# Two raw tiles and six weight slots in place of three and five, in the feed-forward stages of a decoder trunk

## The chip, the cores and the metric

The kernel runs on one core of a Trainium2 chip. The metric is the device time of one execution in microseconds; lower is better. The time of a kernel is the median of its runs. Times inside an execution come from one profiled execution and are counted from the start of its span.

PE is the matmul engine (TensorE), DVE VectorE, ACT ScalarE, POOL GpSimd, and SP the engine whose queue issues most of the DMAs. Each engine works through its own instructions in a fixed order.

## The reference

Two decoder layers over 256 positions of width 2048. Layer 0 mixes with sliding-window attention beside an mLSTM memory, layer 1 with a forgetting attention. Each layer then has a SwiGLU feed-forward stage with 5632 hidden columns, which is what this change touches:

```python
h = h + mix.astype(h.dtype)
h = h + swiglu(rms_norm(h, norm_ffn[layer]), w_gate[layer], w_up[layer], w_down[layer])

def swiglu(xn, w_gate, w_up, w_down):
    return (jax.nn.silu(xn @ w_gate) * (xn @ w_up)) @ w_down
```

All inputs are float32.

## The kernel before

**Split products.** A float32 operand is split in two parts, `hi` (a cast by ACT to the matmul's own format) and `lo` (the rest, a subtraction by DVE). A product is then three matmuls, hi x hi, hi x lo and lo x hi (`three`, L557 to L559, and L244 to L246 in `gemm`). Every weight is loaded once from HBM by SP into a raw tile (L145), cast by ACT and subtracted by DVE into a weight slot, and read by PE from there.

**Plain pairs and seven-product pairs.** A feed-forward stage works in groups (`pair_group`): two weight blocks of 512 columns at a time, gate and up or two neighbouring blocks of the down weight, over a list of pairs of 128 input rows. The list `ORDER` gives the kind of each pair by position: 0, 2, 4, 6 and 7 are plain, 1, 3 and 5 are seven-product pairs. A plain pair takes two raw tiles of two blocks (128x1024, tag `raw`, four buffers), two weight slots and 24 matmuls. A seven-product pair treats rows, columns and halves of the positions as a 2x2 block product and forms it with seven block products (Strassen-Winograd) instead of eight: 21 matmuls, but more work on DVE. Its four blocks come into one raw tile of four blocks (`quad()`, L638). Three of them are split straight into a `triple` (ACT's cast of 128x1536 at L380, DVE's `lo` at L381; there are two triples); then DVE forms differences in place in the raw tile (L645, L648, L649), and the results go by two more splits (128x1024 each) into two weight slots, `h1` and `h0` (L650 to L652). The raw tile is read last by the subtraction for `h0`.

**Slots and raw tiles.** Outside the feed-forward stage, the pool `wp` (six buffers, tag `hi`) gives weight slots one at a time. For the stage, `close_layer` takes all six: five go into `stock`, around which `slot()` goes in turn, and the sixth, `own` (L807), serves as a four-block raw tile. Two more raw tiles (`QUADS`, tag `quad`) stand in the stage's own pool; `quads` is the ring of the three, with `own` first. So the first seven-product pair of each layer uses `own`, the second and third the two other tiles. One buffer with tag `quad` first holds a block of the residual stream that is transposed by DMA (`scrap`, n = 1, L374).

**What stands before the stage.** `out_proj` (L535) computes the output projection in four column blocks; its weight chunks use the same six slots. Each finished block is added to the residual stream (`add_out`, L395), copied by ACT (L338), transposed by SP's DMA (L340), joined by ACT (L345) and split into the stage's input `xh`, `xl` (L386, L387). The joins of the last two blocks are issued inside the first group of the stage, behind the cast of the pairs at positions 3 and 5 (`LATER`, `run_due`).

**Order.** The order of each engine's instructions is not written out by hand. The program gives a priority (its own order), and a planner that runs a model of the machine's timeline puts each instruction where the model finds its inputs and buffers ready. So a tile that is free early may be loaded early. After that the order is fixed.

Of the kernel before, what the change touches and what calls it, by code (L numbers as in the profile page):

```python
# [7 lines left out]
F32 = mybir.dt.float32  # L8
BF16 = mybir.dt.bfloat16
F32R = mybir.dt.float32r  # L10
# [7 lines left out]
P = 128  # L18
# [5 lines left out]
NB = 512  # L24
CK = 2
# [29 lines left out]
QUADS = 2  # L55
# [13 lines left out]
def mixed_of(order):  # L69
    return [p for w, p in order if w]  # L70
# [5 lines left out]
def trunk(  # L76
# [26 lines left out]
    wp = ctx.enter_context(tc.tile_pool(name="wp", bufs=6))  # L103
    stock, triples, quads = [], [], []

    def slot():
        if not stock:
            both = wp.tile([P, 2, CK, NB], F32R, tag="hi", name="hi")
            return [both[:, a, :, :] for a in range(2)]
        stock.append(stock.pop(0))  # L110
        return stock[-1]
# [423 lines left out]
    def out_proj(w, idx, key, extra):  # L535
        last, rest = KT - 4, []
        for n0 in (0, 2):
            accs = [new_acc() for _ in range(2)]
            for i in range(2):
                gemm(accs[i], m_of, w, (n0 + i) * NB, NB, 0, last, KT, step=6 * i)  # L540
            for i in range(2):
                gemm(accs[i], m_of, w, (n0 + i) * NB, NB, last, KT, KT, step=6)
                add_out(accs[i], n0 + i)
                (later if n0 == 0 else rest).append(
                    (LATER[n0 + i], split_turned(idx, n0 + i, *scrap(extra[3], n0 + i), extra))
                )
                square_sum(key, n0 + i)
        return rest
# [247 lines left out]
    def close_layer(layer, w_out, idx, key, **rest):  # L796
        with tc.tile_pool(name=f"fp{layer}", bufs=2) as fp:
            junk_of[:] = fp, "tmp", 2
            nx = len(mixed_of(ORDER))
            nd = max(len(mixed_of(o)) for o in DOWN.values())  # L800
            sx = [fp.tile([P, nx, 4, P], F32R, name=f"sx{i}", bufs=1) for i in range(2)]
            x4 = fp.tile([P, 2, P], F32R, name="x4", bufs=1)
            todo = out_proj(w_out, idx, key, (*sx, x4, fp))
            sd = [fp.tile([P, nd, 4, P], F32R, tag=f"sd{i}", name=f"sd{i}", bufs=1) for i in range(2)]
            triples.extend([fp.tile([P, 3, NB], F32R, name=f"{a}{i}", bufs=1) for a in ("hi", "lo")] for i in range(2))
            stock.extend([slot() for _ in range(5)])
            own = wp.tile([P, 2, CK, NB], F32R, tag="hi", name="raw").rearrange("p a k n -> p (a k) n").bitcast(F32)  # L807
            quads.extend([own] + [fp.tile([P, 2 * CK, NB], F32, tag="quad", name="raw", bufs=QUADS) for _ in range(QUADS)])
            ffn(layer, fp, sx, x4, sd, key, todo, **rest)
            stock.clear()  # L810
            triples.clear()
            quads.clear()
# [3 lines left out]
    hi, lo = slot()  # L816
# [368 lines left out]
    for n in range(4):  # L1185
        nc.gpsimd.dma_start(h[:, :, n * NB : (n + 1) * NB], xv[:, :, n * NB : (n + 1) * NB])

    close_layer(0, w_out_even[0], 2, "f0", idx_next=1, key_next="m1")


    r1 = rstd("m1")
    wi1 = w_in_odd[0]
    with tc.tile_pool(name="od", bufs=1) as od:
# [80 lines left out]
        for i in range(4):  # L1274
# [23 lines left out]
            elif i < 3:  # L1298
                n = NB if i == 1 else VT
# [32 lines left out]
    def finish(acc, n, gf):  # L1332
        for t in range(NT):
# [31 lines left out]
            nc.scalar.dma_start(ov[:, t, NB : 2 * NB], b1)  # L1365

    close_layer(1, w_out_odd[0], 3, "f1", finish=finish)


# [47 lines left out]
```

## Time and profile before

| | us |
|---|---|
| median of 3 runs | 2092.7 (2092.03 to 2093.31) |
| profiled execution | 2090.63 |
| its span | 2088.8 |
| PE busy | 2072.2 (99%) |
| DVE busy | 1806.2 (86%) |
| ACT busy | 1368.3 (66%) |
| span, feed-forward stage of layer 0, first product matmul | 328.03 |
| the same, layer 1: start of the first cast for it on ACT that PE waits for | 1389.82 |

A row of a timeline gives start, length, engine, line, operation, the tiles written and read, shapes, and a count where equal instructions are joined; in brackets stands the idle time of the engine before it and what ended it. Busy time of PE is modelled from pipelined matmuls, each shown some 0.39 us long though the next one starts 0.23 us after it; where PE runs without a stop is seen from the distance between starts. "SPq" is the issue of a DMA by SP, not its transfer.

### The profile page before, as it was taken

The numbers are of one execution on the slowest core, as the hardware profiler recorded it, in microseconds if no ns is written. First come the engines' busy times: TensorE is split into PE (matmuls) and PEld (weight loads), VectorE is DVE, ScalarE is ACT, GpSimd is POOL, SyncE is SP. The second block draws the span as 40 slices with busy tenths as digits, with TensorE's granted clock in tenths as the row PEclk, the third lists the DMA queues.
The fourth block names the chain that finished last, engine by engine and source line by source line (L and its number), as shares of the span: only waits on it lengthen the run. The fifth ranks groups of instructions, "written<-read, shape, count | busy, mean of one in ns | idle before, by whom it ended". The sixth has DMA issues, their size and how long they took to land.

```text
span 2088.8 us, 26467 instructions
## 1 busy us (share of the span) xinstructions
PE 2072.2 (99%) x9473; PEld 1715.1 (82%) x9473; DVE 1806.2 (86%) x2169; ACT 1368.3 (66%) x1649; POOL 44.1 (2%) x69
## 2 busy tenths in 40 slices
PE   9999999999999999999999999999999999999998
PEld 7878887888888888888888888878888888888887
DVE  6788767999999989998899688679989999999984
ACT  6777677665577646667677676577655667556763
POOL 1010000000000000000000001000000000000000
PEclk9999999999999999999999999999999999999999
DMA  8566577766677666666676776586756766666754
GB/s 292 175 206 195 189 240 195 236 205 197 206 216 229 211 193 223 219 209 185 204 205 214 223 202 183 156 255 217 237 186 196 232 197 217 226 206 200 235 157 159
DMA packets 309571, 434.84 MB, mean 208 GB/s; under 512 B 106412, under 2 KB 114624, under 8 KB 309312
## 3 DMA queue, kind: packets, MB, share of 16 engines
q1 hardware_dynamic: 307088, 426.27, 65.3%
q0 software_dynamic: 1632, 5.80, 0.9%
q8 instruction: 74, 1.21, 0.2%
q10 hardware_dynamic: 720, 1.09, 0.1%
q14 instruction: 57, 0.47, 0.1%
HBM read 408.68 MB, written 2.12 MB: 197 GB/s over the span
## 4 chain that ended last, share of the span: by engine, by line
PE 91%; ACT 3%; DMA 2%; DVE 2%; issue 1%; SPq 0%; POOL 0%; POOLq 0%; ACTq 0%; DVEq 0%
PE acc L558 21%; PE acc L557 20%; PE acc L559 20%; PE prod L557 5%; PE prod L558 5%; PE prod L559 5%; PE acc L245 4%; PE acc L244 4%; PE acc L246 4%; PE p L411 1%; ACT box L345 1%; DMA box<-box 1%; DVE hi L207 1%; PE po L512 0%; DMA raw<-in_w_up_dram 0%
## 5 line engine op out<-in xcount | busy, mean ns | idle before, releaser
L206 ACT CAST hi<-raw 128x1024 fp32r<-128x1024 f32 (+3 forms) x561 | 568.2, 1025 | 361.6 <-PE acc L559 194.3
L207 DVE TENSOR_TENSOR hi<-raw,hi 128x1024 fp32r<-128x1024 f32 (+3 forms) x561 | 659.4, 1188 | 129.2 <-ACT hi L206 127.1
L559 PE MATMUL acc<-hi,xl 128*128 128x512 f32 x1320 | 512.4, 390 | 0.0
L557 PE MATMUL acc<-hi,xh 128*128 128x512 f32 x1320 | 495.8, 391 | 4.8 <-ACT hi L206 4.5
L380 ACT CAST hi<-raw 128x1024 fp32r<-128x1024 f32 (+2 forms) x299 | 345.8, 1170 | 230.4 <-PE acc L559 195.1
L558 PE MATMUL acc<-hi,xh 128*128 128x512 f32 x1254 | 487.7, 390 | 0.4 <-DVE hi L207 0.4
L557 PEld LDWEIGHTS acc<-hi,xh 128*128 128x128 f32 x1320 | 247.5, 188 | 58.7 <-ACT hi L206 6.2
L559 PEld LDWEIGHTS acc<-hi,xl 128*128 128x128 f32 x1320 | 247.9, 188 | 51.7
L558 PEld LDWEIGHTS acc<-hi,xh 128*128 128x128 f32 x1254 | 235.5, 188 | 49.9 <-DVE hi L207 0.8
L381 DVE TENSOR_TENSOR hi<-raw,hi 128x1024 fp32r<-128x1024 f32 (+1 forms) x204 | 241.2, 1183 | 10.1 <-ACT hi L380 9.3
L381 DVE TENSOR_TENSOR lo<-raw,hi 128x1536 fp32r<-128x1536 f32 x95 | 166.8, 1755 | 48.1 <-ACT hi L380 46.0
L559 PE MATMUL acc<-hi,ml 128*128 128x512 f32 x466 | 181.0, 389 | 0.0
L557 PE MATMUL acc<-hi,mh 128*128 128x512 f32 x466 | 173.2, 389 | 0.0
L558 PE MATMUL acc<-hi,mh 128*128 128x512 f32 x437 | 170.4, 390 | 0.1
L245 PE MATMUL acc<-hi,mh 128*128 128x512 f32 (+1 forms) x322 | 126.3, 392 | 0.0
L244 PE MATMUL acc<-hi,mh 128*128 128x512 f32 (+1 forms) x322 | 125.8, 391 | 0.0
L246 PE MATMUL acc<-hi,ml 128*128 128x512 f32 (+1 forms) x322 | 123.7, 391 | 0.0
L645 DVE TENSOR_TENSOR raw<-raw 128x1024 f32<-128x1024 f32 x95 | 115.8, 1219 | 0.3
L557 PEld LDWEIGHTS acc<-hi,mh 128*128 128x128 f32 x466 | 87.5, 188 | 18.2
L559 PEld LDWEIGHTS acc<-hi,ml 128*128 128x128 f32 x466 | 87.5, 188 | 18.1
L245 PE MATMUL acc<-hi,xh 128*128 128x512 f32 (+3 forms) x288 | 99.9, 347 | 0.2 <-DVE hi L207 0.2
L246 PE MATMUL acc<-hi,xl 128*128 128x512 f32 (+3 forms) x288 | 99.1, 345 | 0.0
(364 smaller groups left out, 3077.8 us busy)
## 6 DMA issues: line engine op xcount, KB each, us to landing
raw<-in_w_gate_dram SPq DMA_DIRECT2D x176, 512.0 KB, 4.3
raw<-in_w_up_dram SPq DMA_DIRECT2D x176, 512.0 KB, 4.8
raw<-in_w_down_dram SPq DMA_DIRECT2D x176, 512.0 KB, 4.7
raw<-in_w_in_odd_dram SPq DMA_DIRECT2D x88, 512.0 KB, 5.1
raw<-in_w_in_even_dram SPq DMA_DIRECT2D x51, 512.0 KB, 4.8
raw<-in_w_out_even_dram SPq DMA_DIRECT2D x32, 512.0 KB, 5.0
raw<-in_w_out_odd_dram SPq DMA_DIRECT2D x32, 512.0 KB, 4.8
hr<-in_w_in_even_dram SPq DMA_DIRECT2D x12, 512.0 KB, 4.4
```

The source lines that it names most:

```text
L206: latest[0] = nc.scalar.copy(hi[:, k, 0:n], raw[:, k, 0:n])
L207: nc.vector.tensor_tensor(out=lo[:, k, 0:n], in0=raw[:, k, 0:n], in1=hi[:, k, 0:n].bitcast(F32), op=ALU.subtract)
L244: nc.tensor.matmul(o, ah[:, ts], hi, start=(k == 0), stop=False)
L245: nc.tensor.matmul(o, ah[:, ts], lo, start=False, stop=False)
L246: nc.tensor.matmul(o, al[:, ts], hi, start=False, stop=(k == k_all - 1 and cs.stop == n))
L345: nc.scalar.copy(ju[:, :, b], turned[:, b, :, :, :].rearrange("p k t q -> p (k t q)"))
L380: cast = nc.scalar.copy(dst_h, src)
L381: nc.vector.tensor_tensor(out=dst_l, in0=src, in1=dst_h.bitcast(F32), op=ALU.subtract)
L557: nc.tensor.matmul(o, ah, hi, start=start, stop=False)
L558: nc.tensor.matmul(o, ah, lo, start=False, stop=False)
L559: nc.tensor.matmul(o, al, hi, start=False, stop=stop)
L645: nc.vector.tensor_tensor(out=raw[:, 1:4:2, :], in0=raw[:, 3:4, :].broadcast_to([P, 2, NB]), in1=raw[:, 1:3, :], op=ALU.subtract)
```

## The change

`own` goes: the sixth buffer of `wp` becomes a sixth weight slot in `stock`, and the ring of four-block raw tiles has the two of the stage's pool alone. The first seven-product pair takes the first of these, the second pair the second, the third pair the first again, and so on.

```diff
-            stock.extend([slot() for _ in range(5)])
-            own = wp.tile([P, 2, CK, NB], F32R, tag="hi", name="raw").rearrange("p a k n -> p (a k) n").bitcast(F32)
-            quads.extend([own] + [fp.tile([P, 2 * CK, NB], F32, tag="quad", name="raw", bufs=QUADS) for _ in range(QUADS)])
+            stock.extend([slot() for _ in range(6)])
+            quads.extend(fp.tile([P, 2 * CK, NB], F32, tag="quad", name="raw", bufs=QUADS) for _ in range(QUADS))
```

No instruction is added or taken away, and no tile changes its size.

## The prediction

> **What bounds the kernel now.** I read the page first, then the waits of the matmul engine (PE), the table of stretches, and last the timelines of PE, the sync queue (SP), ScalarE (ACT) and VectorE (DVE) where PE is not full. From the page:
>
> ```profile
> span 2088.8 us, 26467 instructions
> ...
> PE 2072.2 (99%) x9473; PEld 1715.1 (82%) x9473; DVE 1806.2 (86%) x2169; ACT 1368.3 (66%) x1649; POOL 44.1 (2%) x69
> ...
> PE 91%; ACT 3%; DMA 2%; DVE 2%; issue 1%; SPq 0%; POOL 0%; POOLq 0%; ACTq 0%; DVEq 0%
> ...
> raw<-in_w_up_dram SPq DMA_DIRECT2D x176, 512.0 KB, 4.8
> ```
>
> PE is busy for all but 16.6 us, and the chain that ended last is 91% PE. The change adds and removes no matmul, so it can only move time in which PE stands still or runs slowly. The table of stretches (start:end, length, then the busy us of PE, weight load, DVE, ACT, POOL with counts, the granted PE clock, DMA share, GB/s) shows where that is:
>
> ```profile
> 323.00:340.00 17.00, 13.13 (x48) 9.44 (x47) 7.97 (x11) 11.14 (x18) 0.69 (x1) 0.90 0.74 122
> 1387.00:1401.00 14.00, 11.43 (x49) 8.50 (x48) 7.74 (x10) 10.61 (x17) 0.71 (x1) 1.00 0.63 139
> 323.00:452.00 129.00, 124.98 (x536) 100.74 (x535) 117.99 (x138) 93.16 (x105) 0.69 (x1) 0.99 0.73 213
> 1384.00:1514.00 130.00, 127.24 (x555) 103.41 (x554) 120.05 (x142) 96.16 (x109) 0.71 (x1) 1.00 0.71 219
> 484.00:656.00 172.00, 172.00 (x760) 142.42 (x759) 162.00 (x171) 103.31 (x101) 0.00 (x0) 1.00 0.67 213
> ```
>
> The first two rows are the first pairs of the two feed-forward stages. In the last row, deep inside such a stage, PE is never idle, at 172.00/760 = 0.226 us from matmul to matmul, while DVE is at 162.00/172.00 = 94%. PE at the two beginnings, rows of its timeline (start, length, in brackets the idle time before and what ended it):
>
> ```profile
> 326.96 0.39 PE L559 MATMUL acc<-hi,xl 128*128 128x512 f32 x1
> 328.03 0.50 PE L557 MATMUL prod<-hi,xh 128*128 128x512 f32 x1 [0.68 <-ACT hi L380]
> ...
> 329.82 0.67 PE L558 MATMUL prod<-lo,xh 128*128 128x512 f32 x1 [0.83 <-DVE lo L381]
> ...
> 333.27 0.46 PE L557 MATMUL acc<-hi,xh 128*128 128x512 f32 x1
> ...
> 334.72 0.40 PE L559 MATMUL prod<-hi,xl 128*128 128x512 f32 x1
> 337.26 0.73 PE L557 MATMUL acc<-hi,xh 128*128 128x512 f32 x2 [2.14 <-ACT hi L206]
> 338.21 0.73 PE L557 MATMUL prod<-hi,sx 128*128 128x512 f32 x2 [0.22 <-ACT hi L380]
> ```
>
> ```profile
> 1392.75 0.39 PE L557 MATMUL acc<-hi,sx 128*128 128x512 f32 x1
> ...
> 1393.49 0.40 PE L559 MATMUL prod<-hi,xl 128*128 128x512 f32 x1
> ...
> 1396.46 0.39 PE L559 MATMUL prod<-hi,xl 128*128 128x512 f32 x1
> 1399.18 0.73 PE L557 MATMUL acc<-hi,xh 128*128 128x512 f32 x2 [2.33 <-ACT hi L206]
> 1400.13 0.73 PE L557 MATMUL prod<-hi,sx 128*128 128x512 f32 x2 [0.22 <-ACT hi L380]
> ```
>
> Lost time is the distance between two starts less 0.226 us for each matmul step between them. Stall (a), the first product of a seven-product pair waiting for its weights: layer 0, 334.72 - 326.96 = 7.76 for 18 steps (4.07), lost 3.7; layer 1, 1393.49 - 1392.75 = 0.74 for 2 steps, lost 0.3. Stall (b), the next chunk waiting for ACT: 338.21 - 334.72 = 3.49 for 3 steps, lost 2.8; layer 1, 1400.13 - 1396.46 = 3.67 for 3 steps, lost 3.0. Together (a) 4.0 and (b) 5.8, 9.8 us.
>
> **What holds those two places.** SP's timeline, then ACT's, with the two rows of layer 1 last:
>
> ```profile
> 292.85 0.82 SPq L145 DMA_DIRECT2D raw<-in_w_gate_dram  x1
> ...
> 306.43 0.37 SPq L145 DMA_DIRECT2D raw<-in_w_gate_dram  x1
> ...
> 317.21 0.88 SPq L145 DMA_DIRECT2D raw<-in_w_gate_dram  x2
> 318.14 1.62 SPq L145 DMA_DIRECT2D raw<-in_w_up_dram  x2
> ```
>
> ```profile
> 305.82 1.47 ACT L380 CAST hi<-raw 128x1536 fp32r<-128x1536 f32 x1
> ...
> 326.50 1.48 ACT L380 CAST hi<-raw 128x1536 fp32r<-128x1536 f32 x1 [3.22 <-DMA raw<-in_w_up_dram]
> ...
> 331.25 2.56 ACT L345 COPY box<-box 128x1024 uint16<-128x1024 uint16 x2 [2.65 <-DMA box<-box]
> ...
> 336.18 1.03 ACT L206 CAST hi<-raw 128x1024 fp32r<-128x1024 f32 x1
> 337.11 1.04 ACT L380 CAST hi<-raw 128x1024 fp32r<-128x1024 f32 x1
> ...
> 1389.82 1.48 ACT L380 CAST hi<-raw 128x1536 fp32r<-128x1536 f32 x1 [2.16 <-DMA raw<-in_w_up_dram]
> ...
> 1398.10 1.03 ACT L206 CAST hi<-raw 128x1024 fp32r<-128x1024 f32 x1
> ```
>
> A cast of 128x1536 opens a seven-product pair. The one that PE waits for at 328.03 ran at 326.50, on loads issued at 317 to 319: it is the first pair's, whose raw tile `own` is a weight slot and so comes free only as the out projection gives slots back. The cast at 305.82, on loads issued from 292.85 on, is that of a later pair in the tile that was free all along. The pair needed first is loaded last. Behind it ACT, whose order is fixed, runs the join of a transposed block (331.25, after 2.65 us of waiting), and only then the cast of the next plain chunk (336.18) and the first pair's second cast (337.11), for which PE stands.
>
> **The change, part by part.** *The first pair takes the free tile.* Its loads move to where 292.85 stands, its cast to where 305.82 stands, over 20 us ahead of PE's use: late loads cost nothing then. The second pair takes the other tile, which first carries an earlier transposed block; the loads from 306.43 on are the ones that waited for it, so it too is free over 15 us before PE begins the stage. Stall (a) goes: -4.0. What hides the load is the end of the out projection.
>
> *Stall (b).* With the first pair split early, and with a sixth slot instead of one held as a raw tile, the second cast and the next chunk need no slot that waits for that pair. I expect them ahead of the join. At best all 5.8 goes. What is late next is DVE: 117.99 us of work stand in the 129 us of layer 0 and 120.05 in the 130 of layer 1. If DVE can be no fuller than the 94.2% of the stretch where PE never waits, these stretches can shrink to 117.99/0.942 = 125.3 and 120.05/0.942 = 127.4, by 3.7 and 2.6, together 6.3 instead of 9.8. Between 6.3 and 9.8 I take the middle, 8.0: (a) whole, 4.0 of (b).
>
> *A third raw tile less, later on.* Rows of one group of eight pairs in the middle of a stage, from SP, ACT, DVE and PE:
>
> ```profile
> 852.97 0.37 SPq L145 DMA_DIRECT2D raw<-in_w_gate_dram  x1
> ...
> 894.45 1.08 SPq L145 DMA_DIRECT2D raw<-in_w_down_dram  x2
> ...
> 903.17 6.29 SPq L731 DMA_TRANSPOSE turned<-c  x4
> ```
>
> ```profile
> 869.11 2.46 ACT L380 CAST hi<-raw 128x1536 fp32r<-128x1536 f32 x2 [0.98 <-PE acc L559]
> 879.31 1.49 ACT L380 CAST hi<-raw 128x1536 fp32r<-128x1536 f32 x1 [0.98 <-PE acc L559]
> ```
>
> ```profile
> 893.20 1.22 DVE L381 TENSOR_TENSOR hi<-raw,hi 128x1024 fp32r<-128x1024 f32 x1
> ...
> 905.17 1.22 DVE L381 TENSOR_TENSOR hi<-raw,hi 128x1024 fp32r<-128x1024 f32 x1
> ```
>
> ```profile
> 902.00 0.39 PE L557 MATMUL prod<-hi,sx 128*128 128x512 f32 x1
> ```
>
> One tile is loaded at 852.97, cast at 869.11, read last until 893.20 + 1.22 = 894.42, and loaded again at 894.45: 41.5 us, one group, so three tiles are all held all the time. Of that, 25.3 us lie between cast and last read, and 16.1 before the cast, of which a load needs 4.8. Even if all three pairs of a group held a tile for 25.3 + 4.8 = 30.1 us, or 27.1 + 4.8 = 31.9 like the one cast at 879.31 (to 906.39), two tiles would be asked for 3 x 30.1 = 90 of 83 us: the cast must then come some 2.5 us later per pair. It can, since PE uses the pair cast at 869.11 only around 897 to 902. So I put this at nothing; its cover is that lead, and the second rival prices its loss. Nothing below zero is possible here, as PE has no idle time in such groups.
>
> *The sixth slot, later on.* It lets the splits run further ahead; PE is already full there: nothing.
>
> **A rule weighed.** From 329.82 to 333.27 PE takes 3.45 us for 8 steps, twice 0.226 each, and the granted clock of that stretch is 0.90: some 1.6 us of (a) are a halved clock, right behind 0.68 + 0.83 us of idling. I let it go with the stall; the third rival is that it stays. The Trainium skill, "TensorE: Matmul & The Clock Gate", Part 1 (The HAM clock gate), says that the clock halves after at least one idle window of about 3.4 us; by that rule the gaps here are too short to be the cause. The trace agrees with the length of the window, but the idling ahead of it is 1.5 us.
>
> **The sum.** -4.0 - 4.0 = -8.0. The profiled execution took 2090.63 us, 1.8 around its span, and would take 2082.6; the runs' median is 2092.7, 2.1 higher, so the forecast is 2084.7.
>
> **Rivals.** *The join keeps its place.* ACT's order is made with the first pair moved, and still sets the join and its wait ahead of the chunk at 336.18. For it: the order of both layers is the same, and in layer 1 the pair came nearly in time (0.3 lost) and (b) was still 3.0. Against it: the slot that the chunk needs comes earlier. Then only (a) goes: 2092.7 - 4.0 = 2088.7, just within 0.2%, which is about what a measurement of this kernel can tell from no change.
>
> *Two raw tiles are too few (slower).* Place: each gate and up group. A tile last read until 906.39 finds SP in transposes from 903.17 to 909.46; its load lands 4.8 later, 914.3, while the next group's cast, 41.5 after 869.11, stands at 910.6. ACT waits 3.7 us, and all behind it. DVE is free for 5.8% of 41.5 = 2.4 us a group and makes up no more: 1.3 of lead is lost per group. The lead of the last parts is 902.00 - 894.42 = 7.6, gone after about five groups; the other six of the eleven groups of each layer pay 1.3: 12 x 1.3 = 15.6, or 2100.3 us. It decides from a wait of 2.4 us per group. Against it: a cast may wait without hurt while PE's use is 25 us off, if the order of ACT puts other work first.
>
> *The slow clock stays.* If the halved stretch does not come from the two gaps, it stays when they go: 1.6 of (a) are not gained, 2086.3 us. For it: two gaps of 2.14 and 2.33 us, longer ones, are followed by normal steps. Against it: it begins at the very matmul that ends the second gap.
>
> **How the numbers follow.** Forecast 0.50, slow clock 0.10, join 0.20, too few tiles 0.20. So faster 0.60, same 0.20, slower 0.20. The forecast's own range, the slow clock in it, is 2081 to 2088.4: the low end is all of 9.8 gone and 1.9 for small stalls and the spread of the runs, the high end the edge of 0.2%. For 8 in 10 it reaches past the join, to 2098, most of the way to the second rival, leaving out some 0.15 above and 0.05 below.
>
> **What would show it.** Right: the first gate load of each stage is followed by the cast that PE's first product uses; no PE idle over 0.3 us at either beginning; no halved clock there; the plain cast ahead of the join on ACT. Wrong: PE waits for ACT behind the join (first rival); ACT waits for loads before casts of 128x1536 in every group, and PE idle time in the middle of the stages, now none (second rival).

## The result, and the profile after

The changed kernel takes 2101.0 us (median of 5 runs, 2098.9 to 2103.9) against 2092.7 us: the ratio is 1.0044, 95% interval 1.0033 to 1.0054. It is slower, where 2084.7 us was forecast.

The profiled execution after took 2098.87 us, the fastest of the five, with a span of 2097.1 us. From its page:

```profile
span 2097.1 us, 26429 instructions
...
PE 2075.4 (99%) x9473; PEld 1714.4 (82%) x9473; DVE 1804.0 (86%) x2169; ACT 1355.3 (65%) x1649; POOL 44.2 (2%) x69
...
PE 65%; DVE 17%; DMA 7%; issue 6%; ACT 4%; SPq 0%; ACTq 0%; DVEq 0%; POOLq 0%; POOL 0%
```

PE has the same 9473 matmuls and is still busy 99% of the span. What is new is the chain that ended last: 65% PE where it was 91%, with 17% DVE and 7% DMA in it. The work that sets the end now runs through raw tiles and splits. The table of stretches says where. Its columns are start:end, length, the busy time of PE, weight load, DVE, ACT and POOL with counts, the granted clock, DMA share and GB/s. First the kernel before, in stretches that the prediction did not show, then the changed kernel:

```profile
323.00:345.00 22.00, 18.13 (x70) 13.57 (x69) 12.97 (x20) 16.14 (x24) 0.69 (x1) 0.92 0.71 129
345.00:1010.00 665.00, 664.81 (x2936) 548.87 (x2935) 620.73 (x661) 427.20 (x436) 0.00 (x0) 1.00 0.66 209
...
1384.00:1410.00 26.00, 23.43 (x101) 18.45 (x100) 17.67 (x25) 22.19 (x30) 0.71 (x1) 1.00 0.70 190
1410.00:2000.00 590.00, 589.79 (x2602) 487.04 (x2601) 555.07 (x592) 374.13 (x375) 0.00 (x0) 1.00 0.67 212
```

```profile
323.00:345.00 22.00, 22.00 (x99) 18.22 (x98) 16.54 (x25) 20.24 (x30) 0.69 (x1) 1.00 0.68 206
345.00:1010.00 665.00, 656.51 (x2873) 537.70 (x2872) 608.58 (x650) 412.38 (x427) 0.00 (x0) 0.99 0.65 205
1384.00:1410.00 26.00, 26.00 (x116) 21.52 (x116) 22.11 (x31) 22.10 (x31) 0.70 (x1) 1.00 0.62 165
1410.00:2000.00 590.00, 586.38 (x2580) 482.38 (x2579) 542.66 (x579) 365.51 (x370) 0.00 (x0) 1.00 0.66 212
```

At both beginnings PE is now never idle (22.00 of 22.00, 26.00 of 26.00). In the rest of the two stages, full before, it now stands still for 8.5 and 3.6 us. Counted much as in the prediction, from the distances between matmul starts beyond 0.227 us (only distances over 0.232 us count), the whole execution loses 34.2 us where it lost 25.9. The difference of 8.3 us is that of the spans, and it splits like this:

| lost time of PE, us | before | after |
|---|---|---|
| first pairs, layer 0 (323 to 345) | 6.6 | 0.0 |
| first pairs, layer 1 (1384 to 1405) | 3.4 | 0.0 |
| rest of the stage, layer 0 (345 to 1000) | 2.0 | 14.1 |
| rest of the stage, layer 1 (1405 to 1996) | 1.6 | 6.5 |
| all else | 12.3 | 13.6 |

The waits of ACT show what took the place of the old ones. The columns are engine, line and what it waited for: us in all, times, longest. The kernel before, then the changed one:

```profile
ACT hi L380 <- PE acc L559: 195.4, 139, 5.5
...
ACT hi L380 <- DMA raw<-in_w_up_dram: 5.4, 2, 3.2
```

```profile
ACT hi L380 <- DMA raw<-in_w_up_dram: 124.1, 37, 7.0
...
ACT hi L380 <- DVE raw L649: 79.5, 33, 9.3
...
ACT hi L380 <- DVE raw L645: 57.7, 40, 3.9
...
ACT hi L380 <- DMA raw<-in_w_down_dram: 39.8, 20, 4.5
...
ACT hi L380 <- PE acc L559: 19.2, 13, 3.9
```

Before, the casts of the seven-product pairs waited for PE to give something back: the splits were ahead. Now they wait 164 us in 57 waits for loads, and the second and third casts of a pair another 137 us for DVE to form the differences. PE's own waits in the changed kernel, in the same columns:

```profile
PE acc L558 <- DVE hi L207: 3.1, 6, 0.7
PE prod L557 <- DVE xl L387: 2.9, 1, 2.9
PE acc L557 <- ACT hi L206: 1.7, 3, 1.0
...
PE prod L558 <- DVE lo L381: 1.1, 2, 0.9
PE prod L558 <- DVE hi L381: 0.6, 2, 0.4
```

L206 and L207 are the splits of plain chunks, which stand behind the late splits of the pairs (L380, L381) in the queues of ACT and DVE. So PE waits more for a plain chunk than for the pair itself (4.8 us against 1.7). One turn of one raw tile in the changed kernel, in a down group of layer 0, from DVE, SP and ACT:

```profile
689.49 1.21 DVE L381 TENSOR_TENSOR hi<-raw,hi 128x1024 fp32r<-128x1024 f32 x1
...
709.55 1.23 DVE L381 TENSOR_TENSOR hi<-raw,hi 128x1024 fp32r<-128x1024 f32 x1 [0.55 <-ACT hi L380]
```

```profile
690.73 0.88 SPq L145 DMA_DIRECT2D raw<-in_w_down_dram  x2
...
710.81 0.98 SPq L145 DMA_DIRECT2D raw<-in_w_down_dram  x2
```

```profile
696.58 2.43 ACT L380 CAST hi<-raw 128x1536 fp32r<-128x1536 f32 x2 [4.52 <-DMA raw<-in_w_down_dram]
...
720.42 1.49 ACT L380 CAST hi<-raw 128x1536 fp32r<-128x1536 f32 x1 [2.05 <-DMA raw<-in_w_down_dram]
```

```profile
701.04 0.50 PE L558 MATMUL prod<-hi,sd 128*128 128x512 f32 x1 [0.41 <-DVE hi L381]
702.85 0.74 PE L557 MATMUL acc<-hi,mh 128*128 128x512 f32 x2 [0.17 <-ACT hi L206]
712.64 0.50 PE L557 MATMUL acc<-hi,mh 128*128 128x512 f32 x1 [0.42 <-ACT mh L380]
```

The last subtraction that reads the tile ends at 689.49 + 1.21 = 690.70; SP issues the next loads into it at 690.73; the cast, standing ready, waits 4.52 us and starts at 696.58; the last reader ends at 710.78 and the next load goes out at 710.81. There is no gap in the loop but the way of the load. Put together from the rows of 69 of the 95 pairs for which both loads could be told apart, a raw tile goes through 0.9 us from its last read to the issue, 6.4 us to the landing of both halves, 0.4 us to the cast and 19.4 us from cast to last read: 27.1 us. Two tiles for three pairs make 27.1 x 3/2 = 40.6 us, about the 41.5 us of PE's group of eight pairs. A turn that includes its waits comes out near the period in any case; what tells is that only 0.9 + 0.4 = 1.3 us of it are waits. Before, for 45 pairs, the same four parts are 0.3 + 5.9 + 15.3 + 20.3 = 41.8 us for three tiles: a landed tile had 15.3 us to spare before its cast. These 45 pairs are held for a shorter time than the rest. Over all 95 pairs it is 23.9 us from cast to last read before and 20.0 after, which leaves a reserve nearer to 12 us before.

### The profile page after: what moved, and what is told of

Read it like the earlier page. It is cut to its first block, busy times and chain, and to the rows that moved or that the text cites. A ratio compares the mean times of both kernels' runs of the same rounds, so it can differ in the third digit from the quotient of the medians.

```text
span 2097.1 us, 26429 instructions
## 1 busy us (share of the span) xinstructions
PE 2075.4 (99%) x9473; PEld 1714.4 (82%) x9473; DVE 1804.0 (86%) x2169; ACT 1355.3 (65%) x1649; POOL 44.2 (2%) x69
## 3 DMA queue, kind: packets, MB, share of 16 engines
q8 instruction: 74, 1.21, 0.2%
## 4 chain that ended last, share of the span: by engine, by line
PE 65%; DVE 17%; DMA 7%; issue 6%; ACT 4%; SPq 0%; ACTq 0%; DVEq 0%; POOLq 0%; POOL 0%
PE acc L558 12%; PE acc L559 12%; PE acc L557 12%; PE acc L245 6%; PE acc L244 6%; PE acc L246 5%; DVE hi L207 4%; DMA raw<-in_w_up_dram 4%; PE prod L557 3%; DVE hi L381 3%; PE prod L559 3%; PE prod L558 3%; DMA raw<-in_w_down_dram 3%; ACT hi L380 2%; DVE raw L645 2%
## 5 line engine op out<-in xcount | busy, mean ns | idle before, releaser
L207 DVE TENSOR_TENSOR hi<-raw,hi 128x1024 fp32r<-128x1024 f32 (+3 forms) x561 | 658.5, 1186 | 116.6 <-ACT hi L206 114.0
L206 ACT CAST hi<-raw 128x1024 fp32r<-128x1024 f32 (+3 forms) x561 | 563.1, 1021 | 248.0 <-PE acc L559 81.5
L380 ACT CAST hi<-raw 128x1024 fp32r<-128x1024 f32 (+2 forms) x299 | 345.9, 1166 | 344.4 <-DMA raw<-in_w_up_dram 124.1
L381 DVE TENSOR_TENSOR hi<-raw,hi 128x1024 fp32r<-128x1024 f32 (+1 forms) x204 | 240.4, 1179 | 11.4 <-ACT hi L380 11.4
L381 DVE TENSOR_TENSOR lo<-raw,hi 128x1536 fp32r<-128x1536 f32 x95 | 166.5, 1753 | 72.3 <-ACT hi L380 72.1
L557 PEld LDWEIGHTS acc<-hi,mh 128*128 128x128 f32 x466 | 87.3, 188 | 20.3 <-ACT hi L206 1.2
L558 PEld LDWEIGHTS acc<-hi,mh 128*128 128x128 f32 x437 | 82.0, 188 | 23.3 <-DVE hi L207 6.2
```

The source lines that it names most:

```text
L206: latest[0] = nc.scalar.copy(hi[:, k, 0:n], raw[:, k, 0:n])
L207: nc.vector.tensor_tensor(out=lo[:, k, 0:n], in0=raw[:, k, 0:n], in1=hi[:, k, 0:n].bitcast(F32), op=ALU.subtract)
L380: cast = nc.scalar.copy(dst_h, src)
L381: nc.vector.tensor_tensor(out=dst_l, in0=src, in1=dst_h.bitcast(F32), op=ALU.subtract)
L557: nc.tensor.matmul(o, ah, hi, start=start, stop=False)
L558: nc.tensor.matmul(o, ah, lo, start=False, stop=False)
```

## The experiments

Theory A: two raw tiles are too few, and the early tile for the first pair is a gain by itself. Theory B: the planner's order, once the first pair is moved, is what costs. Rival C: the sixth slot is what costs.

**Three tiles, the early one first.**

```diff
-            quads.extend([own] + [fp.tile(...) for _ in range(QUADS)])
+            two = [fp.tile(...) for _ in range(QUADS)]
+            quads.extend([two[0], own, two[1]])
```

> Three raw tiles and five weight slots as before; only the order of the ring is changed: the tile that is free early, then the slot `own`, then the other tile. Theory A (two tiles are too few: a tile comes free so late that its load lands behind the place where the next cast could stand; the early tile for the first pair is a gain by itself): the stalls of about 10 us at the two beginnings shrink by 4 to 10 us and nothing else changes, 2083 to 2089 us. Theory B (the planner's order as a whole, once the first pair is moved, is what costs; the number of tiles does not matter): as slow as the changed kernel, 2097 to 2104 us.

Measured: 2091.6 us, ratio 0.9998 (0.9988 to 1.0008). Neither theory said this. The stall is not gone, it has moved to the second pair, whose tile is now the late slot. SP, ACT and PE of this kernel:

```profile
322.51 0.37 SPq L145 DMA_DIRECT2D raw<-in_w_gate_dram  x1
...
334.31 0.58 SPq L145 DMA_DIRECT2D raw<-in_w_up_dram  x1
```

```profile
338.96 1.48 ACT L380 CAST hi<-raw 128x1536 fp32r<-128x1536 f32 x1
```

```profile
340.49 0.50 PE L557 MATMUL prod<-hi,xh 128*128 128x512 f32 x1 [1.42 <-ACT hi L380]
342.28 0.50 PE L558 MATMUL prod<-lo,xh 128*128 128x512 f32 x1 [0.83 <-DVE lo L381]
```

The two halves of `own` are loaded at 322.51 and only at 334.31, with DMA transposes in between, and PE waits again. The place of the slot in the ring decides who is late. Theory B is weakened, since the steady part (between 420 and 1000 and between 1480 and 1996) stayed nearly as it was: it lost 1.9 us, where the kernel before loses 1.2 and the changed kernel 18.5.

**Three tiles, the slot last.** This keeps the first two pairs where the change puts them.

```diff
-            quads.extend([own] + [fp.tile(...) for _ in range(QUADS)])
+            quads.extend([fp.tile(...) for _ in range(QUADS)] + [own])
```

> As before, with the ring in the order early tile, other tile, `own`: the first two pairs stand as in the changed kernel, and a third tile still exists. Theory A: 2083 to 2087 us, the beginnings free of stalls as in the changed kernel and no waits of the 128x1536 casts for loads to speak of (before: 5 us in all). Theory B: 2097 to 2104 us.

Measured: 2085.3 us, ratio 0.9970 (0.9958 to 0.9981): faster than both kernels. Its stretches and its waits for loads:

```profile
323.00:345.00 22.00, 22.00 (x98) 18.21 (x98) 16.58 (x25) 20.89 (x32) 0.69 (x1) 1.00 0.78 235
345.00:1010.00 665.00, 663.24 (x2927) 547.07 (x2926) 618.60 (x660) 421.05 (x429) 0.00 (x0) 1.00 0.65 207
1384.00:1410.00 26.00, 26.00 (x116) 21.56 (x115) 19.37 (x32) 23.76 (x35) 0.70 (x1) 1.00 0.78 241
1410.00:2000.00 590.00, 587.64 (x2588) 484.07 (x2588) 551.30 (x584) 368.66 (x366) 0.00 (x0) 1.00 0.66 210
```

```profile
ACT hi L380 <- DMA raw<-in_w_up_dram: 4.1, 6, 1.7
```

Both beginnings are full, as in the changed kernel, and the waits for loads are as small as before. So the gain at the beginnings is there, 6.3 us of it net, since the rest of the two stages loses 8.5 us where it lost 3.6 before. What the changed kernel gave away beyond that goes with the third tile. Theory B falls as it was put. One thing stays untested: the planner makes the order of the instructions anew for every kernel, and in the traces ACT, DVE and SP work in another order with two tiles than with three. No run holds that order fixed, so the missing tile and the order that the planner makes for two tiles are not told apart.

**Two tiles, five slots.**

```diff
-            stock.extend([slot() for _ in range(6)])
+            stock.extend([slot() for _ in range(5)])
```

> The changed kernel with five weight slots in place of six; the sixth buffer stays unused. Two raw tiles. Theory A: the waits of the 128x1536 casts for loads stay (160 us in the changed kernel), and with a slot less there is less lead to cover them: 2101 to 2112 us. Rival C (the sixth slot is what costs, since it lets plain chunks run ahead of the seven-product pairs): 2083 to 2092 us.

Measured: 2097.4 us, ratio 1.0027 (1.0016 to 1.0038). The loss is there without the sixth slot, so C falls; but it is not larger than the changed kernel's, so A's "less lead" missed too. To price the slot, both were run again side by side:

> The changed kernel once more, beside the next one on the same chip, to price the sixth slot. Theory A (two raw tiles in turn are a loop of their own: free, issue, load, cast, hold until the last read, some 27 us for two tiles and three pairs in 41 us, as long as PE's own group): 2098 to 2103 us.

> Two raw tiles and five slots, as e3_five_two, beside the changed kernel. If the sixth slot covers part of the lost lead, 2 to 6 us more than the changed kernel; if the loop over the raw tiles alone sets the pace, the same within 2 us; e3_five_two was 1.0027 of the kernel before and the changed kernel 1.0044, so 2 to 4 us less is what these two looks say.

Measured: the changed kernel 2100.7 us, ratio 1.0039 (1.0024 to 1.0054); with five slots 2096.6 us, ratio 1.0025 (1.0015 to 1.0035). Five slots were 3.6 and 4.0 us faster in the two comparisons; the intervals overlap. The sixth slot buys nothing where tiles are short. Waits do not explain why. With five slots the casts wait half as long for loads,

```profile
ACT hi L380 <- DMA raw<-in_w_up_dram: 57.8, 36, 5.3
...
ACT hi L380 <- DMA raw<-in_w_down_dram: 24.6, 16, 2.7
```

82 instead of 164 us, while the turn of a tile is as long (0.8 + 6.6 + 0.9 + 19.7 = 28.0 us) and PE loses nearly as much between 420 and 1000 and between 1480 and 1996 (15.8 for 18.5). So the sum of these waits does not measure the loss, and what five slots gain here stays open.

**Shorter loads.** The changed kernel, with each load of a four-block tile cut to half, then to a quarter, of its columns (`NB // 4` in both places). The rest of each tile is zero and left out of the result.

```diff
-                    load_raw(w, k0, c0, NB, into=raw[:, CK * m : CK * (m + 1), :])
+                    load_raw(w, k0, c0, NB // 2, into=raw[:, CK * m : CK * (m + 1), :])
...
+            for q in quads:
+                nc.gpsimd.memset(q[:, :, NB // 2 : NB], 0.0)
```

> The changed kernel, two raw tiles and six slots, with each load of a four-block tile cut to half of its columns (the other half of the tile is set to zero once and stays zero, so half of the seven-product weights are left out of the result); all work of ACT, DVE and PE stays. Theory A: a tile is loaded in less time, the casts wait less for loads, and a large part of the loss goes: 2084 to 2092 us. Theories B and C: 2097 to 2104 us, as the order, the slots and the tiles are those of the changed kernel.

> As e4_half_loads with a quarter of the columns loaded (three quarters of each four-block tile stay zero, left out of the result). In the trace of the changed kernel a load takes 6.4 us from issue to landing on average, with half of the columns 4.6, and PE's lost time in the feed-forward stages behind their beginnings went from about 19 to 10 us. Theory A: still shorter loads lose still less, 2081 to 2086 us. If the load is not what closes the loop, no less than e4_half_loads, 2087 us.

Measured: 2087.2 us, ratio 0.9979 (0.9969 to 0.9988), and 2085.4 us, ratio 0.9966 (0.9953 to 0.9979). Waits of the casts for loads, half and then quarter:

```profile
ACT hi L380 <- DMA raw<-in_w_up_dram: 60.0, 28, 5.2
...
ACT hi L380 <- DMA raw<-in_w_down_dram: 3.8, 5, 1.5
```

```profile
ACT hi L380 <- DMA raw<-in_w_up_dram: 35.3, 20, 5.5
...
ACT hi L380 <- DMA raw<-in_w_down_dram: 3.4, 2, 1.9
```

From issue to the landing of both halves a tile needs 6.4, 4.6 and 3.9 us with whole, half and quarter loads; the waits are 164, 64 and 39 us; PE loses 18.5, 10.0 and 8.3 us between 420 and 1000 and between 1480 and 1996. With two tiles, six slots and 1.8 us less of loading, 14 us of the run are back. Loads of a quarter bring the two tiles to the time of three, 2085.3 us. This is the strongest case for A, that the loop over the tiles closes through the load. It is not free of the rival above: the order of ACT, DVE and SP differs here too from that of the changed kernel.

**A slot less where tiles are not short.** The kernel with `own` last, with four slots in place of five.

```diff
-            stock.extend([slot() for _ in range(5)])
+            stock.extend([slot() for _ in range(4)])
```

> Three raw tiles with `own` last, as e2_own_last, and four weight slots in place of five; the sixth buffer stays unused. It prices a slot where raw tiles are not short. If the splits' lead of a slot (16 slots in 41 us, so 2.6 us each) is needed, PE waits where the leads were smallest: 2088 to 2100 us. If slots are not short either: 2084 to 2087 us, as e2_own_last.

Measured: 2090.4 us, ratio 0.9992 (0.9982 to 1.0002), 0.22% or some 4.6 us more than with five (0.9970). With three tiles a slot has a price between five and four; with two tiles it has none between six and five.

**Less to do for a tile.** The two kernels without the in-place differences.

```diff
-                nc.vector.tensor_tensor(out=raw[:, 1:4:2, :], ...)
-                nc.vector.tensor_tensor(out=raw[:, 2, :], ...)
-                nc.vector.tensor_tensor(out=raw[:, 0, :], ...)
```

> The changed kernel without the three in-place differences of each four-block tile (L645, L648, L649: 1.2 + 0.7 + 0.7 us of DVE for each of 95 pairs, left out of the result): the second and third cast need the load alone, so a tile is held for a shorter time. If the loop load, cast, hold, free over two tiles is what costs, shortening its other part does what shorter loads did: hold down from 19.4 us by 3 or more, 2082 to 2090 us. If only the load's own lateness counts: 2096 us or more.

> The same left out of the kernel with three raw tiles and `own` last (e2_own_last, 2085.3 us), as a control for the 250 us of DVE work that goes too: with three tiles neither DVE nor the tiles hold PE back, so it gains 0 to 3 us, 2081 to 2086 us. If DVE's work as such is the limit in both, the gain is like that of the kernel with two tiles, 8 us or more, which PE's own work does not leave room for: 2078 us or less.

Measured: two tiles 2077.7 us, ratio 0.9930 (0.9915 to 0.9945); three tiles 2078.5 us, ratio 0.9936 (0.9919 to 0.9952). One stretch of each, two tiles first:

```profile
345.00:1010.00 665.00, 665.00 (x2945) 550.78 (x2944) 520.64 (x525) 422.40 (x439) 0.00 (x0) 1.00 0.67 208
```

```profile
345.00:1010.00 665.00, 665.00 (x2944) 550.35 (x2943) 522.19 (x526) 424.83 (x438) 0.00 (x0) 1.00 0.65 207
```

PE is full in both, and two tiles are as good as three. But the control gained about 7 us, not 0 to 3. So the in-place work costs some time even with three tiles; that it does so through a DVE that is nearly full (618.60 of 665 us in the kernel with `own` last) is likely, but not shown. And over all pairs the time from cast to last read fell from 20.0 to 17.7 us only, less than the 3 us or more that were expected; what nearly went were the waits for loads (12 us where the changed kernel has 164). So this pair of runs does not tell a shorter hold from a less busy DVE. It shows that the price of the third tile is gone once this work on DVE is.

## Why the prediction was wrong

*Stall (a) and stall (b): right.* Both went, whole: 10.0 us, by the mechanism given. The first pair's cast (128x1536) and the join in the changed kernel, from ACT's timeline:

```profile
305.18 1.47 ACT L380 CAST hi<-raw 128x1536 fp32r<-128x1536 f32 x1
...
317.59 1.05 ACT L380 CAST hi<-raw 128x1024 fp32r<-128x1024 f32 x1
318.84 1.06 ACT L380 CAST hi<-raw 128x1024 fp32r<-128x1024 f32 x1 [0.20 <-DVE raw L649]
...
325.90 1.04 ACT L206 CAST hi<-raw 128x1024 fp32r<-128x1024 f32 x1
...
330.96 2.58 ACT L345 COPY box<-box 128x1024 uint16<-128x1024 uint16 x2
```

The pair's three casts and the next plain chunk's (325.90) all stand ahead of the join (330.96). The 1.8 us of the 9.8 that were held back for DVE were gained too; the first rival (the join keeps its place) did not happen. The third rival (the slow clock stays) did not either: the granted clock between 323 and 345 is 1.00. A halved clock came up at another place, from 997.85 to 1004.67, behind the new waits at the end of layer 0's stage, where matmuls start 0.427 us apart and it costs some 2 us.

*"A third raw tile less, later on ... I put this at nothing": this step failed.* The rows were read rightly: three tiles always held, two asked for 90 of 83 us, so the cast must come later by some 2.5 us per pair. What was wrong is the next sentence, that the lead of 25 us covers it. That lead is not a stock to be spent once. It is what the third tile makes: with two, most casts come when a load lands, a load goes out when a tile is given back, and the tile is given back only after splits that wait in DVE's queue. The splits of a pair, and those of the plain chunks behind them, then end when PE is about to use them. In the example above the cast starts at 696.58 and PE already stands at 701.04. Followed back from wait to wait, eight of the thirteen losses above 0.4 us in the rest of the two stages (6.0 of 13.0 us) come to a load that went out when a tile was given back. For the other five, the largest single loss below among them, this path is not shown. Also, 4.8 us for a load is the time of one issue; a tile has two, and both land 6.4 us after the first issue. The term of 0 measured 17.0 us (3.6 to 20.6 in the table), against 10.0 gained. Of these 17.0 us, 12.1 are lost only with two tiles (20.6 against the 8.5 us with `own` last); the other 4.9 are lost with three tiles too, and why stays open.

*"Nothing below zero ... PE has no idle time in such groups"* was right, and the same sentence should have warned: such a group has no reserve that a longer wait could use up unseen, DVE being at 94%.

*The second rival* (two raw tiles too few, 2100.3 us) is what happened, with 0.20 as its chance. Its principle, lead lost faster than DVE wins it back, agrees with the runs. Its place does not: it was put on SP standing in transposes in the gate and up groups, while a freed tile is loaded after 0.9 us on average, and 18.1 of 22.7 us of lost time in the two stages (counted to the end of the slow stretch at 1004.67) fall on matmuls of the down products. The largest single loss stands at the end of layer 0's stage, where the last pairs meet the adds and splits for the next layer:

```profile
996.01 0.50 PE L558 MATMUL prod<-lo,mh 128*128 128x512 f32 x1 [0.95 <-DVE lo L381]
999.62 0.77 PE L557 MATMUL prod<-hi,sd 128*128 128x512 f32 x1 [2.88 <-DVE xl L387]
```

That its price came out within 1 us is partly luck.

*The sixth slot at nothing:* near enough, but with two tiles it cost about 4 us, if anything.

## What to carry to other kernels

When a buffer is taken from a ring, count the turn of one buffer without its waits, from issue to landing and from first use to last read, times uses over buffers, against the period of the engine that sets the pace. Here that is (5.9 + 23.9) x 3/3 = 29.8 of 41.5 us with three tiles, and with the same times (5.9 + 23.9) x 3/2 = 44.7 with two. (With two tiles the time of use came down to 20.0 us, and PE waited.) If the period has no room for it, the lead that seemed to cover it is gone, because the buffer was what made it. A change that moves a buffer and also drops one should be tried as two changes: here the order alone (the late buffer last) gained 0.30% and what came with the smaller ring cost more than that. And where a late buffer stays in a ring, someone gets it: first and second place in the ring were worth nothing, the last place all.

## What the runs showed of the hardware

The halved clock follows short gaps, but not always. Around the same place in two executions of the same kernel, with two tiles and five slots, the first row is of e3_five_two and the second of e6_five_two_again:

```profile
995.00:1005.00 10.00, 6.46 (x27) 4.25 (x26) 8.14 (x14) 8.62 (x13) 0.00 (x0) 1.00 0.40 116
```

```profile
995.00:1005.00 10.00, 7.55 (x25) 4.77 (x24) 8.01 (x13) 10.00 (x15) 0.00 (x0) 0.83 0.30 103
```

PE idled 3.5 us in the first, in gaps of 2.40 and 0.93 us and a shorter one, at full clock; in the second 2.45 us, with one long gap of 2.30, at a granted clock of 0.83. In the kernel before, gaps of 0.68 and 0.83 us were enough. So the cost of a gap of a microsecond or two is uncertain by about 1.6 us, the price of one slow stretch of 3.4 us (8 matmuls in 3.45 us in the kernel before).

What tells the two executions apart is where the gap lies. The trace's record of the granted clock changes in whole steps of 3.413 us: from its first full-clock entry to the halving there are 324.27 us in the kernel before, 341.33 in e1_free_first and 993.28 in e6_five_two_again and in the changed kernel, which are 95, 100 and 291 steps. In e6_five_two_again the gap of 2.30 us lies inside one step (995.92 to 999.34), and the next step is slow. In e3_five_two a step ends at 998.97, within the gap of 2.40 us, and leaves 1.5 us of idling in one step and 1.1 in the next. In the twelve profiled executions, between the first and the last matmul, five full-speed steps are followed by a slow one; PE stood idle for 1.5 to 2.7 us in each of them. No step with less than 1.5 us of idling was followed by a slow one. Three steps with 1.5 to 1.7 us (two in the kernel before, one in e3_five_two) were not either, so the idle time alone does not settle it there.

The Trainium skill, "TensorE: Matmul & The Clock Gate", Part 1 (The HAM clock gate), has the window run freely, whatever the kernel does; the traces agree, as nearly the same gap halves the clock in one execution and not in the other. They do not agree with its idle window of about 3.4 us as the condition: a step with 1.5 us of idling was enough.
